# A hybrid attention and convolution layer on one core: the depthwise convolution in three half-length parts, and the work around it moved

## The chip, the cores and the metric

The kernel runs on one core of one Trainium2 chip, as one program. The metric is the device time of one execution in microseconds (us); a kernel's time is the median of several runs. TensorE (PE) does the matrix products, VectorE (DVE) and ScalarE (ACT) the elementwise work, GpSimd (POOL) small scalars, and SyncE (SP) issues most of the DMAs.

## The reference

One encoder layer is applied to two sequences that share weights: the prompt with 512 tokens and the sample with 256, both of width 1024. Half of the mixer is an attention with low-rank query and key/value projections (8 heads, 64 plain and 32 rotated dimensions), the other half a convolution over 512 channels:

```python
u = conv_a * jax.nn.sigmoid(conv_g)
u = lax.conv_general_dilated(u, dw_w[:, None, :], window_strides=(1,),
                             padding=[(CONV_PAD, CONV_PAD)],      # 15 on both sides
                             dimension_numbers=("NWC", "WIO", "NWC"),
                             feature_group_count=CONV_CH) + dw_b  # 31 taps, one filter per channel
u = jax.nn.silu(layer_norm(u, conv_ln_g, conv_ln_b))
merged = jnp.concatenate([rms_norm(attn, attn_out_g), rms_norm(u, conv_out_g)], axis=-1)
...
x = x + merged @ w_out
x = x + swiglu(rms_norm(x, norm2_g), w_gate, w_up, w_down)        # 2816 wide
return rms_norm(x, final_g)
```

## The kernel before

The 768 tokens are six blocks of 128: 0 to 3 the prompt's, 4 and 5 the sample's. Every value that enters a matrix product is split into a rounded high part, cast by ACT, and a low remainder, subtracted by DVE (`split`); three products of halves make one, all issued through the helper `mm`.

The order of work. The kernel is written for a scheduler that places each instruction on its engine by program order as priority, as soon as its inputs and buffers allow by its own estimate; an instruction in `tc.keep_in_program_order` (`pinned` while `pin[0]` is set) is not moved past others of its kind. Each engine then runs its list strictly in order. Buffers come from pools; a pool with `reuse="tile"` lets a new tile wait only for the old tiles that lie in the same memory, one without it for the whole old pool.

The stages, with their time in the profiled execution:

- 0 to 116 us, projection for the convolution: TensorE makes `pc`, in four channel groups of 128; `glu` turns a group into `u`, with padding of zeros at both ends, for each sequence.
- 116 to 161 us, the other projections: queries, keys, values. A query block's rotated dimensions are turned by `rope` on DVE (four instructions a block, into scratch tiles `rc` and `rs` and back to the query tile `sa`).
- 161 to 268 us, attention in 12 units, four pairs of heads for the sample and eight heads for the prompt; `unit_step(i)` overlaps the steps of neighbouring units. The steps are: transposed and split queries (`ptq`, then `qh` by ACT and `ql` by DVE), scores `pss`, row maxima `ngmx` by DVE, the exponential by ACT, transposed probabilities `ptp`, output `po`, `attnT`.
- In between the convolution's taps run on DVE, a multiply-add per tap on a whole row of tokens (`acc<-u,c,acc`). They are not written where they run: `mm` hands some out for every product that it issues, at a rate for each stage (`RATE`).
- After unit `LN0` = 4 come the prompt's convolution norms: `conv_ln` (transposes `pcl`, statistics on DVE, result `z` by ACT), `conv_act1` and `conv_act2` (transposes `pca`, tanh, row sums `prc`), `conv_split`. The attention's own norm is `attn_norm` (transposes `pan` and `pcb`).
- 268 to 303 us, the convolution half of the output projection, `oc(b, o)` for prompt block b and half o (`pe`). The sample's taps, norms and activation stand between these products.
- 303 to 361 us, the attention half, block by block (`both`, `out_attn`), and each block's norm (`x1_norm`) and transposes (`x1_turn`).
- 361 to 812 us, the feed-forward network; the last of its down products that shares a pattern is `p4`. To 843.5 us, a last product (`hd`) and the final norm. The last product's weights `w` arrive in `sr` tiles; ACT casts them to `ra` and `sa` regions, in the same list as `p4`'s casts `wr<-sr`.

Of the kernel before, what the change touches and what calls it, by code (L numbers as in the profile page):

```python
# [27 lines left out]
KW = 31  # L28
# [21 lines left out]
def tile_hybrid_layer(  # L50
# [53 lines left out]

    def split(dst_hi, dst_lo, src, scale=None):
        if scale is None:
            ACT.copy(dst_hi, src)  # L107
            DVE.tensor_sub(dst_lo, src, dst_hi.bitcast(F32))  # L108
# [67 lines left out]
    def wab(cols=1024):  # L176
# [10 lines left out]
    acc = [[accp.tile([128, n], F32, tag=f"acc{s}{i}", name=f"acc{s}{i}") for i in range(4)] for s, (_, n) in enumerate(SEQ)]  # L187
    u = [
        [up.tile([128, n + 2 * PAD], F32, tag=f"u{s}", name=f"u{s}{i}", bufs=4) for i in range(4)]
        for s, (_, n) in enumerate(SEQ)  # L190
    ]
    for s, (_, n) in enumerate(SEQ):
        for t in u[s]:
            POOL.memset(t[:, :PAD], 0.0)
            POOL.memset(t[:, PAD + n :], 0.0)
# [3 lines left out]
    def conv_chunk(i, j):  # L199
# [8 lines left out]
    slab = [  # L208
        [acc[s][k // 2] if k % 2 else u[s][k // 2][:, PAD : PAD + n] for s, (_, n) in enumerate(SEQ)]
        for k in range(8)  # L210
    ]
# [36 lines left out]

    def conv_taps(i, s):

        w = lambda j: c[:, C_DW + i * KW + j : C_DW + i * KW + j + 1]
        n = SEQ[s][1]
        a, us = acc[s][i], u[s][i]
        ACT.activation(a, us[:, :n], AF.Identity, bias=c[:, C_DB + i : C_DB + i + 1], scale=w(0))
        for j in range(1, KW):
            yield n / 512, lambda j=j: DVE.scalar_tensor_tensor(a, us[:, j : j + n], w(j), a, ALU.mult, ALU.add)  # L256
# [49 lines left out]
    def glu(i):  # L306
        for s, (o, n) in enumerate(SEQ):
            t1 = ta.tile([128, 512], F32, tag="t1", name=nm("t1"), bufs=2)
            t2 = ta.tile([128, 512], F32, tag="t2", name=nm("t2"), bufs=2)
            DVE.tensor_mul(t1[:, :n], pcs[i][1][s], rb[:, o : o + n])  # L310
            ACT.activation(t1[:, :n], t1[:, :n], AF.Tanh)
            DVE.tensor_mul(t2[:, :n], pcs[i][0][s], rb[:, o : o + n])
            DVE.scalar_tensor_tensor(
                u[s][i][:, PAD : PAD + n], t1[:, :n], 1.0, t2[:, :n], ALU.add, ALU.mult
            )
            taps[s].append(conv_taps(i, s))
# [54 lines left out]
    def rope(dst, src, b, n, tp):  # L371
# [3 lines left out]
        tcs = tp.tile([128, n, 2, 16], F32, tag=f"rc{n}", name=nm("rc"), bufs=2)  # L375
        tsn = tp.tile([128, n, 2, 16], F32, tag=f"rs{n}", name=nm("rs"), bufs=2)
# [88 lines left out]
    def q_up(b):  # L465
# [9 lines left out]
        for n in range(2):  # L475
            ACT.activation(qt[b][:, n * 384 : (n + 1) * 384], pp[n][:, :384], AF.Copy, scale=fq[:, b : b + 1])
        qr = qt[b].rearrange("p (h d) -> p h d", h=H)[:, :, DN:]
        rope(qr, qr, b, H, cTp)
# [90 lines left out]
    cz = {}  # L569

    def conv_ln(b):
# [12 lines left out]
        z = up.tile([128, CC], F32, tag="u0", name=nm("z"), bufs=4)  # L584
# [558 lines left out]
    gw[0] = wx, wpair(gs[0][:, KB])
    x1_turn(5)
    x1_turn(2)
    out_attn(3, 1, wa[1])
    prep(1)
    x1_norm(3)
    behind = {0: lambda: t_sums(2), 1: lambda: t_sums(0), 2: lambda: t_split2(1), 3: lambda: t_split2(2), 4: lambda: t_split2(0)}
    for f in range(NFILL):  # L1150
# [6 lines left out]
        if f == 0:  # L1157
            x1_turn(3)
# [181 lines left out]
    al, wl = [], []  # L1340
    ra_ = region("ra", 12288, F32R)
    sas = [region(f"sa{i}", NSA, F32R) for i in range(2)]
    wat = [ra_[:, NP * 768 + i * 512 : NP * 768 + (i + 1) * 512] for i in range(7)] + [sa(i * 512, 512) for i in range(15)]
    for q in range(NQ):
        w = w_load(1, 0, q)
        for f, i in pairs(q):
# [4 lines left out]
            tc.keep_in_program_order(ACT.copy(wl[f][0], w[:, i, :]))  # L1351
            DVE.tensor_sub(wl[f][1], w[:, i, :], wl[f][0].bitcast(F32))
# [114 lines left out]
```

## Time and profile before

| | us |
|---|---|
| median of 3 runs (lowest to highest) | 846.23 (844.44 to 848.56) |
| profiled execution | 845.27 |
| its span, first to last instruction | 843.5 |
| mean granted clock of TensorE | 0.986 |
| busy: PE / DVE / ACT / POOL | 813.0 / 716.3 / 435.2 / 74.0 |

Busy time is the time in which an engine has an instruction under way. The granted clock is the share of TensorE's full clock that it was given. What an engine waited for is inferred from the events that released it. TensorE's share of 96% is an average over stages of different kinds; what matters for a change in one stage is what the engines do there.

### The profile page before, as it was taken

The numbers are of one execution on the slowest core, as the hardware profiler recorded it, in microseconds if no ns is written. First come the engines' busy times: TensorE is split into PE (matmuls) and PEld (weight loads), VectorE is DVE, ScalarE is ACT, GpSimd is POOL, SyncE is SP. The second block draws the span as 40 slices with busy tenths as digits, with TensorE's granted clock in tenths as the row PEclk, the third lists the DMA queues.
The fourth block names the chain that finished last, engine by engine and source line by source line (L and its number), as shares of the span: only waits on it lengthen the run. The fifth ranks groups of instructions, "written<-read, shape, count | busy, mean of one in ns | idle before, by whom it ended". The sixth has DMA issues, their size and how long they took to land.

```text
span 843.5 us, 12569 instructions
## 1 busy us (share of the span) xinstructions
PE 813.0 (96%) x4414; PEld 727.1 (86%) x4414; DVE 716.3 (85%) x1314; ACT 435.2 (52%) x888; POOL 74.0 (9%) x111
## 2 busy tenths in 40 slices
PE   7999999799999899999999999999999999999996
PEld 6889998676766678799999999999999988888876
DVE  6499999988689965898999888898988669989985
ACT  7633347678686254784333343433434346456734
POOL 0000430002010201100000000000000000004602
PEclk9999999989799999999999999999999999999999
DMA  8822102300001231368554333444344699963334
GB/s 307 295 62 63 45 20 80 128 1 1 1 1 51 75 101 75 114 204 287 193 193 151 117 127 135 147 143 148 126 150 142 207 328 313 315 199 117 133 113 150
DMA packets 50928, 117.20 MB, mean 139 GB/s; under 512 B 5297, under 2 KB 19761, under 8 KB 50865
## 3 DMA queue, kind: packets, MB, share of 16 engines
q1 hardware_dynamic: 50288, 115.80, 40.7%
q8 instruction: 35, 0.57, 0.3%
q10 hardware_dynamic: 576, 0.59, 0.2%
q14 instruction: 29, 0.23, 0.1%
HBM read 93.96 MB, written 22.41 MB: 138 GB/s over the span
## 4 chain that ended last, share of the span: by engine, by line
PE 78%; DVE 9%; ACT 6%; issue 4%; DMA 2%; POOL 1%; ACTq 0%; POOLq 0%; DVEq 0%
PE bank L299 55%; PE pc L299 8%; PE pss L299 3%; DVE acc L256 3%; PE po L299 3%; PE pq L299 2%; PE pt L299 2%; PE ptp L737 2%; DVE wr L108 1%; ACT ra L463 1%; DMA sr<-wdn 1%; ACT ra L107 1%; ACT sa L720 1%; DVE sa L111 1%; PE ptq L692 1%
## 5 line engine op out<-in xcount | busy, mean ns | idle before, releaser
L299 PE MATMUL bank<-ra,wr 128*128 128x384 f32 x1056 | 186.6, 336 | 0.0
L299 PEld LDWEIGHTS bank<-ra,wr 128*128 128x128 f32 x1056 | 183.4, 188 | 0.0
L299 PE MATMUL bank<-sa,wr 128*128 128x384 f32 x780 | 139.2, 336 | 0.0
L299 PE MATMUL bank<-wr,wr 128*128 128x512 f32 x594 | 135.4, 389 | 1.7 <-ACT wr L107 1.5
L299 PEld LDWEIGHTS bank<-sa,wr 128*128 128x128 f32 x780 | 135.5, 188 | 0.0
L299 PEld LDWEIGHTS bank<-wr,wr 128*128 128x128 f32 x594 | 111.4, 188 | 25.4 <-ACT wr L107 1.9
L256 DVE SCALAR_TENSOR_TENSOR acc<-u,c,acc 128x512 f32<-128x512 f32 (+1 forms) x240 | 132.8, 609 | 0.1
L107 ACT CAST wr<-vt 128x512 fp32r<-128x512 f32 x88 | 54.6, 621 | 101.1 <-PE bank L299 98.5
L107 ACT CAST wr<-sr 128x512 fp32r<-128x512 f32 x106 | 64.8, 617 | 63.5 <-PE bank L299 60.4
L108 DVE TENSOR_TENSOR wr<-sr,wr 128x512 fp32r<-128x512 f32 x106 | 71.7, 680 | 16.5 <-ACT wr L107 16.5
L1246 POOL TENSOR_SCALAR fme<-fms 128x1 f32<-128x1 f32 x6 | 24.6, 4107 | 418.7 <-ACT vt L1236 418.5
L108 DVE TENSOR_TENSOR wr<-vt,wr 128x512 fp32r<-128x512 f32 x88 | 59.9, 682 | 0.0
L299 PE MATMUL pc<-ra,sa 128*128 128x512 f32 (+1 forms) x288 | 53.6, 347 | 5.9 <-ACT ra L110 5.9
L299 PEld LDWEIGHTS pc<-ra,sa 128*128 128x128 f32 x288 | 45.5, 194 | 13.0 <-ACT ra L110 6.4
L107 ACT CAST wr<-ra 128x384 fp32r<-128x384 f32 x51 | 26.1, 512 | 34.9 <-PE bank L299 19.9
L299 PE MATMUL pss<-ra,qh 96*128 96x512 f32 (+1 forms) x96 | 31.3, 413 | 7.3 <-ACT qh L107 6.0
L108 DVE TENSOR_TENSOR wr<-ra,wr 128x384 fp32r<-128x384 f32 x51 | 28.2, 553 | 9.1 <-ACT wr L107 8.0
L299 PE MATMUL bank<-wr,ra 128*128 128x512 f32 x144 | 34.8, 396 | 0.0
L299 PE MATMUL pq<-sa,ra 128*128 128x384 f32 x108 | 33.9, 341 | 0.0
L717 DVE TENSOR_REDUCE ngmx<-pss 128x1 f32<-128x512 f32 (+1 forms) x40 | 27.0, 685 | 6.4 <-PE pss L299 6.2
L299 PEld LDWEIGHTS bank<-wr,ra 128*128 128x128 f32 x144 | 26.6, 187 | 6.3
L720 ACT ACTIVATE sa<-pss,ngmx 128x512 f32<-128x512 f32 (+1 forms) x48 | 29.3, 620 | 2.2 <-PE ptp L737 1.9
(234 smaller groups left out, 1343.9 us busy)
## 6 DMA issues: line engine op xcount, KB each, us to landing
sr<-wgu SPq DMA_DIRECT2D x52, 512.0 KB, 4.0
sr<-wdn SPq DMA_DIRECT2D x34, 512.0 KB, 4.6
sumd<-xall SPq DMA_DIRECT2D x44, 192.0 KB, 1.9
ra<-sumd SPq DMA_DIRECT2D x44, 192.0 KB, 5.0
actd<-xall SPq DMA_DIRECT2D x11, 384.0 KB, 2.3
xall<-actd SPq DMA_DIRECT2D x11, 384.0 KB, 2.9
st<-wconv SPq DMA_DIRECT2D x7, 512.0 KB, 5.5
xr<-xtok SPq DMA_DIRECT2D x6, 512.0 KB, 4.4
```

Of the source, the lines that this page charges most:

```text
L107: ACT.copy(dst_hi, src)
L108: DVE.tensor_sub(dst_lo, src, dst_hi.bitcast(F32))
L111: DVE.scalar_tensor_tensor(dst_lo, src, scale, dst_hi.bitcast(F32), ALU.mult, ALU.subtract)
L256: yield n / 512, lambda j=j: DVE.scalar_tensor_tensor(a, us[:, j : j + n], w(j), a, ALU.mult, ALU.add)
L299: pinned(PE.matmul(out, lhsT, rhs, start=start, stop=stop))
L463: ACT.copy(t[DN:DQ, h, :], t[DN:DQ, 0, :].bitcast(F32))
L692: PE.transpose(pt[:DQ, o : o + 128], qt[b0 + b][:, h * DQ : (h + 1) * DQ], ident)
L717: DVE.tensor_reduce(mx, ps.rearrange("p (j n) -> p j n", j=m), AX.X, ALU.max, negate=True)
L720: ACT.activation(P[:, js], ps[:, js], AF.Exp, bias=ngmx[:, b0 + b, h : h + 1], accum_out=asum[:, b0 + b, h : h + 1],)
L737: PE.transpose(pt[:, o : o + 128], P[b][:, j * n + kt * 128 : j * n + (kt + 1) * 128], ident)
L1246: POOL.tensor_scalar(fme[b], fms[:, 2 * b + 1 : 2 * b + 2], 1.0, EPS, ALU.mult, ALU.add)
```

## The change

It has six parts.

1. The convolution. A group's row `u` is now stored as two half-length rows, the even and the odd tokens (`u0` and `v1`), both sequences side by side in one tile `uv`. With even taps, odd taps and their sums `cab`, three half-length filters give P (16 taps on `u0`), Q (15 on `v1`) and S (15 on `u0+v1`); even outputs are P + Q, odd ones S - P - Q shifted. The first tap of each is ACT's. The rates are changed with it, and at most 2 instead of 4 taps' worth are handed out at once (`TAPW`).
2. The norms start after unit 7 instead of 4 and follow in consecutive units, the sample's included, which was between the output projections.
3. `q_rope` of the prompt's blocks is written after units 0 and 1 instead of before the first.
4. Five pools of the attention stage get `reuse="tile"`.
5. The blocks after the mixer run 4 0 1 2 5 3 instead of 4 0 1 5 2 3.
6. The splits of the last product's weights are issued after the last cast of `p4`.

```diff
-RATE = {"A": 0.6, "B": 1.4, "C": 0.6, "D": 1.0, "S": 1.0, "F": 1.2}
+RATE = {"A": 0.6, "B": 1.25, "C": 0.3, "D": 1.1, "S": 1.0, "F": 1.2}
-TAPW = 4
-LN0 = 4
+TAPW = 2
+TAPC = 0.81
+LN0 = 7
...
-    def conv_taps(i, s):
-        a, us = acc[s][i], u[s][i]
-        ACT.activation(a, us[:, :n], AF.Identity, bias=..., scale=w(0))
-        for j in range(1, KW):
-            yield n / 512, lambda j=j: DVE.scalar_tensor_tensor(a, us[:, j : j + n], w(j), a, ALU.mult, ALU.add)
+    def conv_taps(i):
+        u0, v1 = half_rows(i, 0), half_rows(i, 1)
+        P, Q, S = pqs[:, :NP_], pqs[:, HP : HP + NP_ - 1], pqs[:, 2 * HP : 2 * HP + NP_ - 1]
+        yield TAPC, lambda: DVE.tensor_add(xs, u0, v1)
+        ACT.activation(P, u0[:, :NP_], AF.Copy, scale=w(0))
+        ACT.activation(Q, v1[:, 1:NP_], AF.Copy, scale=w(1))
+        ACT.activation(S, xs[:, 1:NP_], AF.Copy, scale=ab(0))
...
+        for j in range(1, 16):
+            yield TAPC, lambda j=j: tap(P, u0, j, w(2 * j))
+            if j < 15:
+                yield TAPC, lambda j=j: tap(Q, v1, 1 + j, w(2 * j + 1))
+            yield TAPC, lambda j=j: tap(S, xs, 1 + j, ab(j))
+        yield TAPC, lambda: DVE.tensor_sub(S, S, P[:, 1:])
+        for s, (o, n) in enumerate(SEQ):
+            r = acc[s][i].rearrange("p (n two) -> p n two", two=2)
+            def even():
+                DVE.scalar_tensor_tensor(r[:, :, 0], Q[:, m : m + h], db, P[:, m : m + h], ALU.add, ALU.add)
+            def odd():
+                DVE.scalar_tensor_tensor(r[:, :, 1], S[:, m : m + h], db, Q[:, m : m + h], ALU.add, ALU.subtract)
...
+        if b >= 4:
+            q_rope(b)
...
-    atp, at_close = pool("atp")
+    atp, at_close = pool("atp", reuse="tile")          # tmp, dp, psD, psX as well
...
         unit_step(i)
+        if i < 3:
+            for b in (2 * i, 2 * i + 1) if i < 2 else ():
+                q_rope(b)
...
         elif i == LN0 + 2:
             for k in range(4):
                 conv_act1(0, k)
                 conv_act2(0, k)
-            for b in range(NB):
-                load_x(b)
-        elif i == LN0 + 4:
+            pin[0] = True
+            conv_ln(4)
+            conv_ln(5)
+            pin[0] = False
+        elif i == LN0 + 3:
+            conv_split(0)
+            for k in range(4):
+                conv_act1(1, k)
+                conv_act2(1, k)
             attn_norm(4)
             attn_norm(5)
-            conv_split(0)
-        elif i == LN0 + 7:
+        elif i == LN0 + 4:
             wc0 = conv_w(0)
...
-    oc(0, 1)
-    tap_all(1)
-    oc(1, 1)
-    conv_ln(4)
-    conv_ln(5)
-    oc(2, 1)
-    for k in range(4):
-        conv_act1(1, k)
-    oc(3, 1)
-    for k in range(4):
-        conv_act2(1, k)
-    conv_split(1)
+    for b in range(4):
+        oc(b, 1)
...
+    behind_p4 = last_act[0].ins
...
-            tc.keep_in_program_order(ACT.copy(wl[f][0], w[:, i, :]))
-            DVE.tensor_sub(wl[f][1], w[:, i, :], wl[f][0].bitcast(F32))
+            with tc.issue_after(behind_p4):
+                split(wl[f][0], wl[f][1], w[:, i, :])
```

What this does to the engines' lists is seen at three places. The first is DVE's list just ahead of the first `ql`, the low half of the first transposed queries. `acc<-u` are taps of whole rows, `pqs<-` half-length taps; `rc`, `rs` and, in the new kernel, `st` are the scratch of a rotation, and `sa` the query tile that it turns. Before:

```order
L256 SCALAR_TENSOR_TENSOR acc_114<-u_122,c,acc_114 128x512
L381 TENSOR_TENSOR rc_1738<-sa_160_1418,c 128x256
L382 TENSOR_TENSOR rs_1739<-sa_160_1418,c 128x256
L256 SCALAR_TENSOR_TENSOR acc_115<-u_123,c,acc_115 128x512
L383 TENSOR_TENSOR sa_160_1418<-rc_1738,rs_1739 128x8x16
L384 TENSOR_TENSOR sa_160_1418<-rc_1738,rs_1739 128x8x16
L256 SCALAR_TENSOR_TENSOR acc_115<-u_123,c,acc_115 128x512
L256 SCALAR_TENSOR_TENSOR acc_116<-u_124,c,acc_116 128x256
L108 TENSOR_TENSOR ql_1785<-ptq_1779,qh_1784 96x512
L108 TENSOR_TENSOR ql_1798<-ptq_1792,qh_1797 96x512
```

The same place now, with the sixth rotation still around the first two `ql`:

```order
L446 TENSOR_TENSOR sa_168_1433<-st_1884 128x8x16
L447 TENSOR_TENSOR sa_168_1433<-st_1884 128x8x16
L290 SCALAR_TENSOR_TENSOR pqs_1578<-uv_114,c,pqs_1578 128x400
L290 SCALAR_TENSOR_TENSOR pqs_1841<-xs_1840,cab,pqs_1841 128x400
L290 SCALAR_TENSOR_TENSOR pqs_1578<-xs_1577,cab,pqs_1578 128x400
L444 TENSOR_TENSOR st_1889<-sa_168_1433,c 128x256
L445 TENSOR_TENSOR st_1889<-sa_168_1433,c 128x256
L290 SCALAR_TENSOR_TENSOR pqs_1841<-uv_115,c,pqs_1841 128x401
L111 TENSOR_TENSOR ql_1777<-ptq_1771,qh_1776 96x512
L111 TENSOR_TENSOR ql_1790<-ptq_1784,qh_1789 96x512
L446 TENSOR_TENSOR sa_168_1433<-st_1889 128x8x16
```

The rotations keep their place, though they are written later; the taps between them are shorter.

The second place is TensorE's list at the end of the convolution half of the output projection, `pe`, up to the first `bank` products. Before, the sample's activation and row sums stand in it:

```order
L299 MATMUL pe_3037<-sa_386_2834,ra_69 128x512 x12
L596 MATMUL pca_3051<-ident,z_3018 128x128
L596 MATMUL pca_3051<-ident,z_3035 128x128
...
L596 MATMUL pca_3075<-ident,z_3035 128x128
L299 MATMUL pe_3082<-sa_386_2834,ra_69 128x512 x12
L299 MATMUL prc_3096<-ones,th_3055 128x2 x4
L299 MATMUL prc_3096<-ones,th_3070 128x2 x4
L299 MATMUL bank_3122<-sa_376_2734,ra_69 128x512 x12
```

Now, with `pcb` the last transposes of an attention norm:

```order
L737 MATMUL pcb_2994<-ident,z_2972 128x128 x4
L737 MATMUL pcb_3007<-ident,z_2972 128x128 x4
L353 MATMUL pe_3020<-sa_411_2893,ra_69 128x512 x12
L353 MATMUL pe_3034<-sa_411_2893,ra_69 128x512 x12
L353 MATMUL pe_3048<-sa_411_2893,ra_69 128x512 x12
L353 MATMUL pe_3062<-sa_411_2893,ra_69 128x512 x12
L353 MATMUL bank_3081<-sa_401_2817,ra_69 128x512 x12
```

The sample's norm and activation have moved into attention, and the projections follow each other.

The third place is ACT's list near the end of `p4`; `wr<-sr` and `wr<-act` are casts for `p4`, `ra<-sr` for the last product. Before:

```order
L107 CAST wr_3211<-act_3940 128x384
L1351 CAST ra_7426<-sr_3217 128x512 x2
L107 CAST wr_3213<-sr_3218 128x512
L107 CAST wr_3215<-act_3940 128x384
L107 CAST wr_3203<-act_3940 128x384
L107 CAST wr_3201<-sr_3219 128x512
L107 CAST wr_3207<-act_3940 128x384
L1351 CAST ra_7426<-sr_3218 128x512 x2
L107 CAST wr_3205<-sr_3219 128x512
L107 CAST wr_3209<-sr_3220 128x512
```

Now:

```order
L110 CAST wr_3160<-sr_3178 128x512
L110 CAST wr_3166<-act_3899 128x384
L110 CAST wr_3164<-sr_3178 128x512
L110 CAST wr_3168<-sr_3179 128x512
L110 CAST ra_7385<-sr_3176 128x512 x2
L110 CAST ra_7385<-sr_3177 128x512 x2
L110 CAST sa_482_7386<-sr_3178 128x512 x2
```

Both pairs of `ra<-sr` casts have moved behind `p4`'s last cast.

More of the change, by code (lines that the diff above doesn't have):

```diff
@@ L185, in tile_hybrid_layer, with half_rows @@
     psA, psA_close = pool("psA", bufs=8, space=PSUM)
[L187 to L195, printed above, removed]
+    HL = [n // 2 + 16 for _, n in SEQ]
+    HO = [0, HL[0]]
+    HW = sum(HL)
+    uv = [accp.tile([128, 2 * HW], F32, tag=f"uv{i}", name=f"uv{i}") for i in range(4)]
+    acc = [[t[:, o : o + n] for t in uv] for o, n in SEQ]
+    HP = 401
+    def half_rows(i, w):
+        return uv[i][:, w * HW : (w + 1) * HW]
     hT = rtiles()
@@ L206, in tile_hybrid_layer @@
     wc[0, 0] = w0
[L208 to L211, printed above, removed]
+    place = [stg.tile([128, 1024], F32, tag="st", name=nm("st"))]
+    place += list(uv)
+    place += [up.tile([128, 3 * HP], F32, tag="pqs", name=nm("xs"), bufs=2) for _ in range(2)]
+    slab = [[p[:, o : o + n] for o, n in SEQ] for p in place]
     t0 = stg.tile([128, 1024], F32, tag="st", name=nm("st"))
@@ L218, in tile_hybrid_layer @@
             nc.sync.dma_start(t0[:, ks], wconv[0, 0][:, ks])
+        if k == 7:
+            p = stg.tile([128, 1024], F32, tag="st", name=nm("st"))
+            slab.append([p[:, o : o + n] for o, n in SEQ])
         for s, (o, n) in enumerate(SEQ):
@@ L226, in tile_hybrid_layer @@
             split(hT[s][0][:, k, :], hT[s][1][:, k, :], slab[k][s], g1[:, k : k + 1])
+    for t in uv:
+        t2_ = t.rearrange("p (w n) -> p w n", w=2)
+        for lo_, hi_ in ((0, 8), (HL[0] - 8, HL[0] + 8), (HW - 8, HW)):
+            POOL.memset(t2_[:, :, lo_:hi_], 0.0)
     wc[1, 0] = conv_chunk(1, 0)
@@ L247, in build_rb @@
             ACT.activation(rb[:, o : o + n], pr[s][:, :n], AF.Copy, scale=0.5)
[L249 to L256 removed]
+    cab = cpool.tile([128, 4, 16], F32, name="cab")
@@ L312, in glu @@
             DVE.tensor_mul(t2[:, :n], pcs[i][0][s], rb[:, o : o + n])
[L313 to L316, printed above, removed]
+            pair = lambda t, w: t[:, :n].rearrange("p (n two) -> p n two", two=2)[:, :, 1 - w]
+            for w in range(2):
+                DVE.scalar_tensor_tensor(
+                    half_rows(i, w)[:, HO[s] + 8 : HO[s] + 8 + n // 2], pair(t1, w), 1.0, pair(t2, w), ALU.add, ALU.mult
+                )
+        taps[0].append(conv_taps(i))
     WTN = [960] * 4 + [768] * 2
@@ L374, in rope @@
         sn = c[:, None, C_SIN + b * 16 : C_SIN + (b + 1) * 16].to_broadcast([128, 2 * n, 16])
-        tcs = tp.tile([128, n, 2, 16], F32, tag=f"rc{n}", name=nm("rc"), bufs=2)
-        tsn = tp.tile([128, n, 2, 16], F32, tag=f"rs{n}", name=nm("rs"), bufs=2)
+        if tp is None:
+            t_ = stg.tile([128, 1024], F32, tag="st", name=nm("st"))
+            tcs, tsn = [
+                t_[:, i * n * 32 : (i + 1) * n * 32].rearrange("p (n two f) -> p n two f", two=2, f=16)
+                for i in range(2)
+            ]
+        else:
+            tcs = tp.tile([128, n, 2, 16], F32, tag=f"rc{n}", name=nm("rc"), bufs=2)
+            tsn = tp.tile([128, n, 2, 16], F32, tag=f"rs{n}", name=nm("rs"), bufs=2)
         s4 = src.rearrange("p n (two f) -> p n two f", two=2)
@@ L569, in tile_hybrid_layer, with z_tile @@
     cz = {}
+    zt = []
+    def z_tile():
+        if not zt:
+            t = up.tile([128, 3 * HP], F32, tag="pqs", name=nm("z"), bufs=2)
+            zt.extend([t[:, : CC], t[:, CC : 2 * CC]])
+        return zt.pop(0)
     def conv_ln(b):
@@ L843, in tile_hybrid_layer @@
         elif i == LN0 + 1:
+            pin[0] = True
             conv_ln(2)
             conv_ln(3)
+            pin[0] = False
+            for b in range(NB):
+                load_x(b)
         elif i == LN0 + 2:
```

52 lines of the change are left out of this document (36 added, 16 removed).

## Prediction

> **What bounds the kernel now.** First the busy line of the page, then the busy time of each engine in stretches cut where the work changes (columns: time, length, then busy microseconds of PE, PEld, DVE, ACT and POOL with their instructions, granted clock, DMA share, GB/s).
>
> ```profile
> PE 813.0 (96%) x4414; PEld 727.1 (86%) x4414; DVE 716.3 (85%) x1314; ACT 435.2 (52%) x888; POOL 74.0 (9%) x111
> 116.00:161.00 45.00, 44.50 (x258) 41.66 (x257) 43.19 (x84) 36.67 (x85) 6.69 (x8) 1.00 0.30 106
> 161.00:176.00 15.00, 7.93 (x42) 6.85 (x41) 13.15 (x27) 4.99 (x15) 0.00 (x0) 0.77 0.00 1
> 176.00:194.70 18.70, 18.29 (x122) 12.18 (x119) 17.50 (x36) 15.62 (x47) 0.00 (x0) 1.00 0.00 1
> 194.70:220.00 25.30, 24.16 (x149) 17.56 (x147) 21.68 (x46) 20.41 (x44) 4.60 (x12) 1.00 0.00 1
> 220.00:232.40 12.40, 11.81 (x44) 9.03 (x45) 7.30 (x16) 8.15 (x19) 1.30 (x2) 0.59 0.01 1
> 232.40:267.70 35.30, 35.22 (x187) 21.12 (x185) 31.89 (x66) 30.25 (x69) 2.60 (x4) 1.00 0.09 31
> 267.70:303.00 35.30, 30.72 (x159) 24.23 (x159) 29.48 (x66) 13.76 (x34) 5.79 (x14) 1.00 0.14 45
> 303.00:308.00 5.00, 5.00 (x16) 3.94 (x15) 3.89 (x8) 4.36 (x8) 1.59 (x2) 0.66 0.42 120
> 308.00:361.00 53.00, 50.94 (x250) 42.09 (x249) 36.94 (x59) 27.79 (x61) 6.71 (x12) 1.00 0.30 109
> 361.00:769.00 408.00, 408.00 (x2231) 392.23 (x2230) 354.98 (x637) 178.63 (x324) 0.00 (x0) 1.00 0.57 191
> 769.00:812.00 43.00, 41.30 (x182) 33.62 (x181) 41.14 (x73) 28.66 (x63) 24.64 (x6) 1.00 0.32 104
> ```
>
> TensorE bounds it: 96% busy overall, without a gap in the 408 us of FFN that the change doesn't touch. Its matmuls are the same after the change, so what can be won is time in which PE is idle or at half clock, and that lies in 161 to 361: idle 7.07 at 161-176 (15.00 - 7.93), 0.41, 1.14, 0.59, 0.08, 4.58 in the output projection's conv half (267.7-303), 0, then 2.06. The clock takes, as busy time times one less the granted clock, 11.81 x 0.41 = 4.8 at 220-232, 5.00 x 0.34 = 1.7 at 303-308, and about 2.4 near 170 (some 5 us of work at half speed). All of it is 25 us, with 1.7 more at 769-812: the ceiling of the gain is 27 us, or 819.
>
> What PE waited for, from the waits (total, times, longest) and the order in time:
>
> ```profile
> ACT qh L107 <- DVE sa L384: 6.2, 1, 6.2
> PE pss L299 <- ACT qh L107: 6.0, 2, 5.7
> 162.45 1.08 PE L692 MATMUL ptq<-ident,sa 128*96 128x128 f32 x8 [0.96 <-ACT sa L476]
> 169.23 1.65 PE L299 MATMUL pss<-ra,qh 96*128 96x256 f32 x6 [5.70 <-ACT qh L107]
> 289.92 1.86 PE L576 MATMUL pcl<-ident,acc 128*128 128x128 f32 x8 [1.22 <-DVE acc L256]
> 295.32 0.33 PE L596 MATMUL pca<-ident,z 128*128 128x128 f32 x1 [0.80 <-ACT z L585]
> 296.19 0.98 PE L596 MATMUL pca<-ident,z 128*128 128x128 f32 x7 [0.55 <-ACT z L585]
> 299.79 0.95 PE L299 MATMUL prc<-ones,th 128*128 128x2 f32 x8
> 300.98 0.61 PE L299 MATMUL prc<-ones,th 128*128 128x2 f32 x4 [0.24 <-ACT th L612]
> 302.20 0.61 PE L299 MATMUL prc<-ones,th 128*128 128x2 f32 x4 [0.62 <-ACT th L612]
> ```
>
> So DVE is late twice: at the first scores (pss) of attention, behind rotations and taps in its queue, and in the output projection, where the sample's taps, LN and activation stand between projections.
>
> **Part 1, the half-length convolution.** Tap prices, by form and, back to back, from the chain:
>
> ```profile
> L256 DVE SCALAR_TENSOR_TENSOR acc<-u,c,acc 128x512 f32<-128x512 f32 x120 | 83.1, 743 | 0.1
> L256 DVE SCALAR_TENSOR_TENSOR acc<-u,c,acc 128x256 f32<-128x256 f32 x120 | 49.9, 475 | 0.0
> 137.56 2.65 DVE acc L256 x4
> 203.28 2.38 DVE acc L256 x6
> L313 DVE SCALAR_TENSOR_TENSOR u<-t,t 128x512 f32<-128x512 f32 x4 | 2.7, 686 | 0.2
> L313 DVE SCALAR_TENSOR_TENSOR u<-t,t 128x256 f32<-128x256 f32 x4 | 1.7, 416 | 0.0
> ```
>
> Back to back a 512-column tap costs 2.65/4 = 0.663 us and a 256-column one 2.38/6 = 0.397, so 1.04 ns a column, and a 401-column tap 0.397 + 145 x 0.00104 = 0.548. Before: 120 x 0.663 + 120 x 0.397 = 127.2 us. After: 4 x 44 = 176 half-length taps = 96.4; 4 sums u0+v1 and 4 subtractions at about 0.5 = 4.0; per group four combinations, 2 of 256 and 2 of 128 columns (0.397 and 0.26) = 1.3, together 5.3; the GLU's second store per tile adds a fixed part, 8 x about 0.1 = 0.8 (its two rows above: 270 ns for 256 columns, so some 146 ns fixed busy, less when queued); tap sums 0.2. Together 106.7, so DVE has 20.5 us less to do. The strided writes of GLU and combinations are in no row; between 0 and double price that is 0 to +8 us of DVE; I take no extra, since the strided rotation writes and reads run beside plain ones at the usual slope. The three ACT starts of 401 columns per group instead of two, and the pad fills on POOL, lie on engines at 52% and 9%.
>
> This is off the path wherever PE doesn't wait. By the order of DVE's instructions, ahead of the first `ql` stand before 118 taps of 512 columns and 1 of 256 (78.6 us), after 131 half taps (71.8), but also 4 sums, 2 subtractions, half the combinations, the GLU's 0.8 and 0.2 (together 6.7), and 5 1/2 rotation pairs instead of 6 (0.4 less). The net is only 0.5 less: the lowered rates of the earlier stages eat the saving by taking fewer taps there, none is left over at the first scores. In the middle of the stage the balance is up to 1.0 against, where PE has 0.5 us of idle in 45. Gain at the first scores: 0.5, between -1.0 and 6 (all the stall).
>
> **Part 2, norms one unit later, and the sample's conv work moved into attention.** DVE needs from the first `ql` to the last combination 10 `ql` and 24 score maxima, 45 half taps (24.7), 2 subtractions (1.0) and 8 combinations (2.6).
>
> ```profile
> L717 DVE TENSOR_REDUCE ngmx<-pss 128x1 f32<-128x512 f32 x32 | 21.7, 685 | 5.3 <-PE pss L299 5.1
> L108 DVE TENSOR_TENSOR ql<-ptq,qh 96x512 fp32r<-96x512 f32 x12 | 8.1, 682 | 3.2 <-ACT qh L107 3.2
> ```
>
> The 34 others at 0.685 x 0.663/0.743 = 0.61 make 20.8, the sum 49.1. From about 169 this is 218, at the earliest, for the LN transposes `pcl(0)` to have their last channel group; before they ran at 194.7. PE has, up to that place in its new order, two units' more work, and the LN transposes and activations that stood there have moved behind; before, PE was busy from 169.2 to 220 for about 5.9 + 18.29 + 24.16 = 48.4, which is 46 at full clock; less some 4 for the transposes that moved behind (32 at 0.13) and some 4 more, since the new place lies a few score groups past 220, it is 46 again, with 2.4 of half clock after the stall: it arrives at about 217. `pcl` is pinned, and behind it in PE's queue stand the next scores, so what DVE is late PE stands still: DVE was 94% busy at 176-194.7, and 49.1/0.94 = 52 gives 221. So a new wait of 1 to 5 us; I take 3.
>
> From there to the first output-projection matmul little DVE work is left. After that matmul PE has the projection, and between its tiles no LN, activation or row sums (the rows at 289.9 to 302.2 above, 5.3 us of matmuls, move ahead into attention). Idle there was 4.58; the waits for LN, activation and row sums go, part of the `pan`/`pcb` waits (about 1) stays: gain 3.6, between 2 and 4.6.
>
> ACT gets denser instead: between `pcl(0)` and the last attention tile it has all LN outputs, activations and softmaxes, where DVE's lag no longer spreads them. At 194.7-267.7 it was busy 20.41 + 8.15 + 30.25 = 58.8 us of 73; less the 20.4 that now lies ahead and with about half of the 13.76 of 267.7-303 added, 45 us of ACT work have some 47 us of PE time. I charge 1 us, between 0 and 6.
>
> The half clock of 220-232 (4.8) comes without an idle stretch, where row sums of two columns, transposes and half-waiting `po` follow each other. These now come later and closer. Nothing says that they disappear: I keep 4.8, between 0 and 9.6.
>
> [...]
>
> First scores to bank stage then: -0.5 (stall) + 3 (new wait) - 3.6 (projection) + 1 (ACT) = -0.1; against it the idle and queueing of 176-220 (0.41 + 1.14) and of DVE-late scores, gone once taps are through, at most 1.5 + 0.6. I take -2.0. And since PE now comes to the bank stage out of uninterrupted projections, not out of idle bits and row sums, the half clock at 303-308 goes: -1.7, between -1.7 and 0. Together -3.8.
>
> **Part 3, deferred rotations.** In program order four blocks' rotations now stand behind the first units, but the order on DVE keeps all but the second half of one ahead of the first `ql`, as before: they are needed by the first units, and DVE had room earlier. They use staging tiles; a weight load that waits for one costs nothing seen at a DMA share of 0.00 to 0.01 up to 232. Zero; the stall of 5.70 stays.
>
> **Part 4, pools that wait by tile.** No row separates a wait for a pool's release. Attention tiles could begin before the last C tile is freed, at most the 0.96 before `ptq`: 0, between 0 and 1.
>
> **Part 5, blocks 4 0 1 2 5 3.**
>
> ```profile
> 351.31 1.09 PE L988 MATMUL bank<-ident,vt 128*128 128x128 f32 x8 [1.56 <-ACT vt L979]
> 359.97 1.09 PE L988 MATMUL bank<-ident,vt 128*128 128x128 f32 x8 [0.51 <-ACT vt L979]
> ```
>
> The transposes of a normed block waited 1.56 and 0.51 for ACT's norm. Each now stands a product later: -1.0, between -2.06 (all idle of 308-361) and +1.
>
> **Part 6, early casts at the end.**
>
> ```profile
> 807.56 1.14 ACT L1351 CAST ra<-sr 128x512 fp32r<-128x512 f32 x2 [2.81 <-DMA sr<-wdn]
> 808.60 1.13 ACT L107 CAST wr<-sr 128x512 fp32r<-128x512 f32 x2
> 809.25 0.69 DVE L108 TENSOR_TENSOR wr<-sr,wr 128x512 fp32r<-128x512 f32 x1 [1.62 <-ACT wr L107]
> 809.27 0.50 PE L299 MATMUL bank<-wr,wr 128*128 128x512 f32 x1 [1.47 <-ACT wr L107]
> 809.99 4.19 PE L299 MATMUL bank<-wr,wr 128*128 128x512 f32 x17 [0.22 <-DVE wr L108]
> ```
>
> PE waits 1.47 + 0.22 for a cast of p4's weights that stands behind two `ra<-sr` casts of the last product, and these wait for a load. With the two (1.14 us) and their wait moved behind, PE can win 1.69 at most; p4's own cast also needs its load, so -1.0, between -1.7 and +0.5 (if the moved casts then hold up the last product, which begins 4 us later).
>
> **The sum.** -3.8 (parts 1 and 2) + 0 + 0 - 1.0 - 1.0 = -5.8. On the profiled execution's 845.27 this is 839.5; that execution lies 0.96 under the median of 846.23, so the median would be 840.4. I take 840.
>
> **The rivals.**
> 1. Large gain: the first scores no longer wait (5.7 and 2.4 of half clock), and the spell of 220-232 goes (4.8). For it: 20.5 us less of DVE work before 218. Against: the order has DVE only 0.5 us lighter at the first `ql`. Then 5.8 + 12.9 = 18.7 less: 827.
> 2. No change: the projection's 3.6 is won, and lost again at the pinned `pcl` (5) and to ACT (2): 844 to 846. For it: 49.1 us of DVE work against 46 of PE.
> 3. Slower: ACT becomes the bound of the last five units. From `pcl(0)` at 221 its 45 us at the 86% at which it ran in 232.4-267.7 are 52.5, PE is done 5.5 later than its own 47, and the spell of half clock that such waits feed doubles (4.8). 840.4 + 5.5 + 4.8 = 850.7. It decides from ACT over 90% busy in the 50 us behind `pcl(0)`, with PE's idle released by ACT.
> [...]
>
> **How the numbers follow.** The forecast (835 to 842) has a chance of 0.45, the large gain (822 to 835) 0.22, no change 0.20 and slower 0.13. The range leaves out a part of the large gain and of the slowest: 824 to 850. About 0.5%, 4.2 us, is what a measurement of this kernel can tell from no change: faster means under 842.0, which is 0.64; slower over 850.5, 0.11; the rest 0.25.
>
> **What would show it.** DVE's busy time falls by about 20 us and PE's stays near 805 to 813. First scores still wait near 169. `pcl` waits for DVE near 218 to 221. From the first projection matmul to the bank stage PE runs with under 1.5 us idle, and the bank stage begins at 299 to 301 instead of 302.7. The clock is 1.00 at the bank's start. No `ra<-sr` cast stands before p4's weights. I am wrong if the first scores come before 166, if PE idles on ACT after `pcl`, or if the clock's cost differs from the 8.9 us of before by over 4.

## The result: slower, and where the time went

The changed kernel takes 853.95 us (median of five executions) against 846.23, a ratio of 1.0073 with a 95% interval of 1.005 to 1.0095. One of the five ran in a slow state, at 1156.24 us and a granted clock of 0.652; the ratio leaves it out, and the median of the other four is 853.25. The forecast was 840. Its profiled span is 852.2 us, 8.7 more than before's 843.5.

The page of the changed kernel, its busy lines; VectorE has 20.3 us less to do than before, and TensorE is busy for 7 us longer with the same 4414 matmuls:

```profile
PE 820.0 (96%) x4414; PEld 732.5 (86%) x4414; DVE 696.0 (82%) x1284; ACT 435.5 (51%) x892; POOL 83.7 (10%) x107
```

The same stretches as in the prediction, of the changed kernel:

```profile
161.00:176.00 15.00, 9.57 (x52) 8.77 (x52) 13.28 (x34) 7.82 (x21) 0.00 (x0) 0.84 0.33 105
176.00:194.70 18.70, 18.22 (x114) 12.94 (x113) 16.73 (x30) 14.12 (x43) 0.00 (x0) 0.95 0.09 29
194.70:220.00 25.30, 25.30 (x140) 16.88 (x136) 22.91 (x41) 19.61 (x48) 0.00 (x0) 1.00 0.00 1
220.00:232.40 12.40, 7.35 (x32) 4.16 (x32) 11.33 (x26) 2.47 (x5) 2.03 (x6) 0.73 0.01 1
232.40:267.70 35.30, 31.20 (x144) 23.64 (x142) 15.65 (x29) 23.92 (x52) 3.82 (x10) 0.74 0.00 0
267.70:303.00 35.30, 32.88 (x169) 22.01 (x169) 18.13 (x32) 26.18 (x59) 6.12 (x15) 0.87 0.19 60
303.00:308.00 5.00, 5.00 (x28) 4.21 (x27) 4.05 (x8) 3.60 (x9) 1.48 (x4) 1.00 0.31 105
308.00:361.00 53.00, 53.00 (x249) 43.54 (x248) 32.12 (x50) 20.95 (x44) 4.05 (x8) 1.00 0.22 80
769.00:812.00 43.00, 43.00 (x191) 35.63 (x190) 41.70 (x74) 28.88 (x64) 24.81 (x4) 1.00 0.38 123
```

In 220 to 232.4 TensorE now idles for 5 us with VectorE busy nearly throughout, and to 303 the clock is far below full. From 303 on there is neither idle nor half clock.

Cut by landmarks of the work, one stretch runs from the first transposed queries (`ptq`) to the first `bank` product, the next from there to the feed-forward network. First the two of before, then the two of the changed kernel:

```profile
162.50:302.70 140.20, 127.30 (x689) 90.50 (x689) 119.35 (x247) 91.48 (x221) 14.29 (x32) 0.94 0.06 19
302.70:390.00 87.30, 85.24 (x433) 75.28 (x434) 68.68 (x113) 53.41 (x109) 8.29 (x14) 0.98 0.45 157
```

```profile
164.30:317.40 153.10, 135.62 (x689) 97.16 (x688) 106.45 (x195) 98.72 (x233) 13.45 (x34) 0.87 0.14 45
317.40:400.80 83.40, 83.33 (x434) 74.21 (x433) 61.59 (x100) 46.60 (x97) 6.91 (x12) 1.00 0.38 134
```

Attention with the projection's conv half is 12.9 us longer, although VectorE does 12.9 us less in it; the stage behind is 3.9 shorter. Up to `ptq` the changed kernel is 1.8 later, which lies within what the first stages differ between profiles of one code (162.5 to 165.8 for before's). The feed-forward network to the first matmul of the last product takes 421.9 (400.8 to 822.7) instead of 424.0 (390.0 to 814.0), and the end is the same 29.5. So 1.8 + 12.9 - 3.9 - 2.1 = 8.7.

Inside the long stretch, the waits of TensorE (total, times, longest), its list at the transposes `pcl`, and the end of VectorE's taps:

```profile
PE pcl L651 <- DVE uv L307: 4.4, 2, 3.4
PE pss L353 <- DVE ql L111: 4.3, 1, 4.3
PE pss L353 <- ACT sa L795: 2.7, 2, 1.6
```

```profile
222.08 0.64 PE L767 MATMUL ptq<-ident,sa 128*96 128x128 f32 x4
223.69 0.30 PE L651 MATMUL pcl<-ident,uv 128*128 128x128 f32 x1 [0.97 <-DVE uv L307]
227.40 1.30 PE L651 MATMUL pcl<-ident,uv 128*128 128x128 f32 x5 [3.40 <-DVE uv L307]
...
226.76 0.75 DVE L307 SCALAR_TENSOR_TENSOR uv<-pqs,c 128x256 f32<-128x256 f32 x2
```

TensorE comes to the transposes of the third group at 222.7 and of the fourth at 224.0; VectorE writes the last of the convolution just before 227.4. The clock in three stretches after that:

```profile
226.00:238.00 12.00, 9.93 (x30) 5.04 (x30) 6.99 (x16) 5.98 (x13) 2.03 (x6) 0.59 0.01 1
250.00:271.00 21.00, 18.30 (x74) 14.39 (x76) 7.57 (x15) 11.90 (x24) 4.04 (x8) 0.59 0.00 1
280.00:288.00 8.00, 7.06 (x28) 4.83 (x28) 3.21 (x7) 5.88 (x13) 1.69 (x4) 0.57 0.00 0
```

As busy time times one less the clock, these cost 4.1, 7.5 and 3.0 us. Such a stretch at half clock is called a spell below.

### The profile page after: what moved, and what is told of

The parts are those of the page before. It is cut to its first block, busy times and chain, and to the rows that moved or that the text cites. A ratio compares the mean times of both kernels' runs of the same rounds, so it can differ in the third digit from the quotient of the medians.

```text
span 852.2 us, 12548 instructions
## 1 busy us (share of the span) xinstructions
PE 820.0 (96%) x4414; PEld 732.5 (86%) x4414; DVE 696.0 (82%) x1284; ACT 435.5 (51%) x892; POOL 83.7 (10%) x107
## 4 chain that ended last, share of the span: by engine, by line
PE 84%; ACT 6%; DVE 4%; issue 3%; POOL 2%; DMA 1%; ACTq 0%; POOLq 0%; DVEq 0%
PE bank L353 58%; PE pc L353 8%; PE pss L353 3%; PE pe L353 3%; PE po L353 2%; PE pq L353 2%; DVE pqs L290 2%; PE ptp L812 2%; PE pt L353 1%; PE prc L353 1%; ACT ra L526 1%; ACT ra L569 1%; POOL r L151 1%; ACT sa L795 1%; PE ptq L767 1%
## 5 line engine op out<-in xcount | busy, mean ns | idle before, releaser
L110 ACT CAST wr<-vt 128x512 fp32r<-128x512 f32 x88 | 54.5, 621 | 89.4 <-PE bank L353 83.4
L1324 POOL TENSOR_SCALAR fme<-fms 128x1 f32<-128x1 f32 x6 | 38.9, 6481 | 415.4 <-ACT vt L1314 415.1
L290 DVE SCALAR_TENSOR_TENSOR pqs<-uv,c,pqs 128x401 f32<-128x401 f32 (+1 forms) x116 | 68.3, 629 | 0.1
L290 DVE SCALAR_TENSOR_TENSOR pqs<-xs,cab,pqs 128x400 f32<-128x400 f32 x60 | 36.4, 629 | 0.2 <-ACT pqs L286 0.2
L353 PE MATMUL pss<-ra,qh 96*128 96x512 f32 (+1 forms) x96 | 33.1, 423 | 3.0 <-ACT sa L795 2.7
```

Source lines behind the costliest of these rows:

```text
L110: last_act[0] = ACT.copy(dst_hi, src)
L290: DVE.scalar_tensor_tensor(d, x[:, o : o + n], sc, d, ALU.mult, ALU.add)
L353: pinned(PE.matmul(out, lhsT, rhs, start=start, stop=stop))
L1324: POOL.tensor_scalar(fme[b], fms[:, 2 * b + 1 : 2 * b + 2], 1.0, EPS, ALU.mult, ALU.add)
```

## The experiments

Theory A: the pinned transposes `pcl` stand too early in TensorE's list for the taps, which end near 227 us; TensorE runs out of other work there, and what follows (half clock, a chain of norm and activation that starts late) comes from that. Theory B: the norm and activation work packed into the last units is dear by itself, for ScalarE and the clock. Runs were timed beside the kernel before on the same chip; its medians there were 847.55, 847.44, 847.39 and 846.39.

### The parts that won (e1)

```diff
 # on the kernel before: both(2) and both(5) exchanged with their x1_turn and x1_norm,
+            with tc.issue_after(behind_p4):
+                split(wl[f][0], wl[f][1], w[:, i, :])
```

> The kernel before with parts 5 and 6 alone (block order 4 0 1 2 5 3, casts of the last product behind p4). By the two traces the changed kernel lost 12.9 us between the first transposed queries and the bank products, and won 3.9 us in the bank stage and 2.1 us at the end of p4. If the two wins come from parts 5 and 6, this kernel wins 1.7 at the end and about 2 in the bank stage (the 1.7 of half clock there belongs to the projection ahead of it and stays): 842 to 843. If the wins only come from another arrival time, nothing: 846.

Measured: 843.84, ratio 0.994 (0.9913 to 0.9968).

```profile
165.80:306.10 140.30, 127.24 (x688) 90.51 (x688) 119.37 (x247) 91.28 (x221) 14.34 (x32) 0.94 0.06 20
306.10:391.30 85.20, 85.12 (x435) 75.48 (x435) 66.55 (x109) 51.97 (x106) 8.54 (x14) 0.98 0.46 153
```

The second stretch is 85.2 instead of 87.3, with no idle, and its half clock (0.98) stays; the first is unchanged. The network takes 422.1 (391.3 to 813.4) instead of 424.0. So in this profile the block order gives 2.1 and the moved casts 1.9; the two were not run one by one. The price of the casts isn't the same in every execution: e8 below has the old ones, and its network takes 422.2 as well (390.1 to 812.3), with no wait for `p4`'s cast.

### One unit later (e2), one more (e6)

```diff
-LN0 = 7
+LN0 = 8      # e6: LN0 = 9, with wc0 = conv_w(0) at the last step
```

> The changed kernel with the norms one unit later still (LN0 = 8). Theory A (the pinned transposes pcl stand too early in TensorE's list, TensorE waits 5.3 us for the last taps, and the half clock that follows the wait costs more): the taps end near 227 and TensorE reaches pcl later by a unit, some 9 us, so the wait goes, with 4 us of half clock: 844 to 848. Theory B (the last units are too full of norm and activation work for ScalarE and for TensorE's clock, whatever the taps do): one unit less to spread it over, the same or worse: 853 to 858.

Measured: 843.25, ratio 0.9929 (0.9901 to 0.9957), 10.7 us under the changed kernel's median.

```profile
165.80:306.40 140.60, 127.67 (x691) 91.62 (x689) 106.05 (x195) 98.63 (x233) 13.49 (x34) 0.94 0.15 49
306.40:389.70 83.30, 83.21 (x433) 74.14 (x432) 62.05 (x101) 47.01 (x98) 6.94 (x12) 1.00 0.38 133
```

No wait for the taps is left at `pcl`; the stretch falls from 153.1 to 140.6, with the same work in the same few units. That is theory A, with a time a little under its range.

> The changed kernel with the norms after unit 9 (LN0 = 9, the output weights' split moved ahead to the last unit). At LN0 = 8 no wait for taps was left, so Theory A sees nothing more to win: 843 to 847, as at LN0 = 8 or a little over. Theory B: each unit later packs the chain tighter, and the last units have no scores to fill it: 848 to 854.

Measured: 847.55, 0.9985 (0.996 to 1.001); the stretch takes 146.3. The time lies between the two ranges. Here B has its share: packed once more, the end of attention costs 5.7 us.

### Fewer taps at the old place (e3)

```diff
-            yield TAPC, lambda j=j: tap(S, xs, 1 + j, ab(j))
+            if i < 2:
+                yield TAPC, lambda j=j: tap(S, xs, 1 + j, ab(j))
```

> The changed kernel without the 28 taps of S in the last two channel groups (that part of the convolution is left out): 15 us less on VectorE, ahead of the transposes pcl, which stay after unit 7. Theory A: the taps end near 212, no wait at pcl, the half clock there goes as well: 843 to 847. Theory B: the stalls behind the transposes stay, only the 5 us wait becomes idle elsewhere: 850 to 854.

Measured: 844.48, 0.997 (0.9935 to 1.0005). The condition takes out 15 taps of VectorE in each of two groups, 30 in all and not 28, which is 16.4 us: S has 16 taps, not 15, and ScalarE does the first. The convolution is written by 210, and `pcl` runs at 221.4 without a wait:

```profile
221.43 1.04 PE L652 MATMUL pcl<-ident,uv 128*128 128x128 f32 x8
...
168.00:310.00 142.00, 128.65 (x689) 93.71 (x688) 89.97 (x165) 98.07 (x233) 13.52 (x34) 0.90 0.15 48
```

142.0 instead of 153.1: with LN0 = 7 kept, 11 of the 12.9 us go when the taps end early.

### The sample's norms put back (e4, e7)

```diff
-            conv_ln(4)
-            conv_ln(5)
...
+    oc(1, 1)
+    conv_ln(4)
+    conv_ln(5)
+    oc(2, 1)      # activation and row sums of the sample follow as before; e7: LN0 = 8 as well
```

> The changed kernel with the sample's norms and activation back between the output projections, where they stood before; the prompt's norms stay after units 7 to 9. Theory A: the wait for the taps at pcl stays with its half clock: 851 to 854. Theory B: ScalarE and the clock have less to carry in the last units, the half clock of 251 to 270 us shortens, and with VectorE free of taps the projection carries the sample's norms without the waits of before: 844 to 848.

Measured: 855.1, 1.0078 (1.005 to 1.0106); the stretch takes 151.6 and the bank stage 85.1. That is the changed kernel's own time: B, with 844 to 848, is out, and A's 851 to 854 is missed by 1.1.

> The changed kernel with LN0 = 8 and the sample's norms and activation between the output projections, where they stood before. Theory A: the sample's place is worth only the small waits on either side: 842 to 846. Theory B: attention's end gets lighter by 5.3 us of matmuls and as much of ScalarE's time, the half clock of 260 to 271 us goes: 838 to 841.

Measured: 846.67, 0.9992 (0.9968 to 1.0015), the stretch 142.9 and the bank stage 85.1 instead of 83.3. Over both expectations: the sample's place among the projections is worse than in attention by 3.4 us (medians) to 4.1 us (the two stretches), 1.7 of it the half clock at the bank stage's start (0.66 in its first 5 us).

### Later norms without the new convolution (e5)

```diff
 # on the kernel before
-LN0 = 4
+LN0 = 7      # attn_norm, conv_split and conv_w moved along
```

> The kernel before with the prompt's norms after units 7, 8 and 9 instead of 4, 5 and 6, and the rest of that chain moved with them; convolution, pools, block order and end as before. Theory A (only the late taps at the pinned transposes made the later norms dear): here the prompt's taps are done by 170 us, so no wait arises at the transposes, and the later norms cost nothing or a little: 844 to 848. Theory B (norm and activation work packed into the last units is dear by itself): 850 to 855.

Measured: 846.92, 0.9996 (0.9967 to 1.0024). The prompt's norms at the changed kernel's place cost nothing where the taps are early. TensorE does wait 3.6 us for taps in this kernel, but for the sample's, among the output projections. And the spell of the kernel before at 220 to 232 is not there: with all of the prompt's transposes and row sums between 200 and 285 the clock stays full.

```profile
200.00:285.00 85.00, 81.25 (x450) 55.72 (x449) 75.16 (x155) 62.85 (x137) 12.39 (x26) 1.00 0.11 32
```

### The convolution without parts 5 and 6 (e9)

```diff
 # on the changed kernel with LN0 = 8: both(5) ahead of both(2) again, and
-            with tc.issue_after(behind_p4):
-                split(wl[f][0], wl[f][1], w[:, i, :])
+            tc.keep_in_program_order(ACT.copy(wl[f][0], w[:, i, :]))
+            DVE.tensor_sub(wl[f][1], w[:, i, :], wl[f][0].bitcast(F32))
```

> The changed kernel with LN0 = 8 and with the old block order and the old end, so that parts 1 to 4 are left with their norms one unit later. If parts 5 and 6 carried the gain of LN0 = 8 (4 us in the kernel before), the convolution's 20 us less of VectorE work is worth nothing in time: 846 to 848, as the kernel before. If the convolution is worth something once it doesn't hold up the transposes: 843 to 845.

Measured: 847.71, 1.0001 (0.9977 to 1.0026). Parts 1 to 4 together, with their norms one unit later, are worth nothing that can be told within a quarter of a per cent. That the twenty microseconds less of VectorE work are worth nothing by themselves is likely but not shown, since parts 2 to 4 are in the same kernel. The bank stage has the old order's idle but full clock:

```profile
305.70:391.40 85.70, 83.64 (x434) 74.16 (x434) 64.24 (x105) 48.97 (x101) 6.72 (x12) 1.00 0.40 137
```

### The first wait moved (e10, e11)

```diff
-RATE = {"A": 0.6, "B": 1.25, "C": 0.3, "D": 1.1, "S": 1.0, "F": 1.2}
+RATE = {"A": 0.6, "B": 1.25, "C": 1.0, "D": 1.1, "S": 1.0, "F": 1.2}
...
+            if len(qsub) > 1:
+                with tc.issue_after(qsub[1].ins):      # the second ql
+                    issue()
...
+                with tc.issue_after(qsub[1].ins):
+                    q_rope(b)
```

> The changed kernel with LN0 = 8, in which the rotations of the prompt's blocks and the taps that are handed out in attention are kept behind the second ql on VectorE (12 taps and 3 rotations fewer ahead of it, about 10 us), rate C 1.0. If the wait of 4.3 us for ql at the first scores is worth its length and the half clock after it (1.9 us): 837 to 840. If VectorE's work up to the last tap bounds the stretch, the wait only moves to the transposes pcl, some 5 us: 843 to 847.

Measured: 846.64, 0.9986 (0.9964 to 1.0008). The wait at the first scores is gone, and the clock with it is full; the first row is LN0 = 8 as it was, the second this kernel:

```profile
161.00:176.00 15.00, 9.54 (x54) 8.76 (x54) 13.96 (x35) 7.77 (x17) 0.00 (x0) 0.86 0.34 106
```

```profile
161.00:176.00 15.00, 12.64 (x86) 11.10 (x84) 9.22 (x22) 10.75 (x26) 0.00 (x0) 1.00 0.11 35
...
PE pcl L656 <- DVE uv L307: 1.6, 1, 1.6
165.80:310.90 145.10, 130.65 (x690) 92.30 (x688) 108.06 (x203) 99.15 (x233) 14.33 (x34) 0.94 0.15 48
```

VectorE was idle for 5.8 of the 15 us, the taps end that much later, `pcl` waits again, and the stretch is 4.5 us longer. The order overshot what it was to test, but the wait did move to the place expected.

> The same with LN0 = 9, so that the transposes stand another unit later. If the first wait moved to the transposes at LN0 = 8, it should have no place here, and the kernel wins 4 to 6 us on LN0 = 9 alone (847.5): 841 to 844. If the packed end of attention is what bounds it then, no gain: 846 to 849.

Measured: 846.98, 0.9995 (0.9962 to 1.0028); the stretch takes 144.9 instead of e6's 146.3. No gain that can be told: the packed end bounds it.

### What brings the half clock (e8, e12)

```diff
 # e8, on the kernel before: row sums of the last channel group alone
+        if i < 3:
+            return
         for b in range(nb):
             mm(pr[:, 2 * b : 2 * b + 2], th[:, b * 128 : (b + 1) * 128], ones[:, :2], ...)
```

> The kernel before with the row sums (prc) of the last channel group alone, those of three of four groups are left out; on TensorE nothing else moves. It asks what sends the clock to half at 222 to 232 us, where TensorE has no idle of over 0.9 us. If the two-column row sums do it, the spell goes (4.8 us) with some 4 us of the matmuls: 836 to 839. If the transposes or nothing in particular does it, only the 4 us: 842 to 843.

Measured: 843.39, 0.9971 (0.9945 to 0.9997), 4.1 us under the kernel before. The spell is still there, 3 us later, and it begins ahead of any row sum:

```profile
220.00:225.00 5.00, 3.38 (x18) 2.25 (x16) 4.70 (x10) 5.00 (x13) 0.00 (x0) 0.98 0.00 0
225.00:230.00 5.00, 5.00 (x16) 2.98 (x15) 3.08 (x7) 2.46 (x5) 1.30 (x2) 0.50 0.01 3
```

```diff
 # e12, on the changed kernel, in conv_ln
+        if b == 0:
+            for _ in range(20):
+                pinned(PE.matmul(pt, kT[0][0][:, 0, :128], kT[0][0][:, 0, :], start=True, stop=True))
```

> The changed kernel with 20 more matmuls of 512 columns (about 4.5 us) ahead of the first transposes pcl, whose results are overwritten: TensorE works in the time in which it waited for the last taps, and nothing else is moved. If the wait itself brings the half clock that follows it (3.7 us at 225 to 240, and through it part of the later spell at 250 to 270), the clock stays at 1.00 there: 848 to 851. If the transposes and the row sums bring it whether TensorE waits or not, the time stays or grows a little: 854 to 857.

Measured: 853.43, 1.0073 (1.0046 to 1.01), the changed kernel's own time.

```profile
219.00:229.30 10.30, 10.24 (x55) 6.91 (x52) 10.30 (x24) 2.36 (x5) 0.00 (x0) 1.00 0.00 1
229.30:250.00 20.70, 17.84 (x96) 11.32 (x95) 11.76 (x22) 16.34 (x36) 4.03 (x12) 1.00 0.00 1
250.00:270.00 20.00, 17.30 (x78) 13.05 (x76) 8.65 (x16) 11.23 (x23) 4.12 (x7) 0.66 0.00 1
```

The extra matmuls fill the wait, and the clock stays at 1.00 until 250: with the wait of 4.4 us goes the half clock of 226 to 238. But the time doesn't fall. The stretch from `ptq` to `bank` takes 152.4 us (165.6 to 318.0) instead of 153.1, though the spell that is gone cost 4.1: TensorE idles for 2.9 us in 229.3 to 250 instead. Counted from `ptq`, the first row sums come only 1.3 us earlier (249.92 less 165.6, against 249.90 less 164.3). So TensorE's pace doesn't bound that part; the norm and activation do. In the changed kernel's chain of what ended last, in order of time:

```profile
238.85 1.29 DVE bst L654 x2
...
240.59 0.56 POOL r L151
...
248.18 0.67 ACT yt L683
...
249.90 1.07 PE prc L353 x8
```

It passes through VectorE's statistics, POOL's power and ScalarE's activations. So theory A stands as to the cause: where the taps end before TensorE comes to `pcl`, by a later place (e2) or by fewer taps (e3), 10.7 and 9.5 us of the median go. How a wait of 4.4 us comes to cost so much is not shown. It is not a late start of the chain alone: in e2 the last group's transposes come later after `ptq`, 68.4 us against 63.1, and what stands behind them takes 72.2 us against 90.0. First e2, then the changed kernel:

```profile
234.20:306.40 72.20, 66.18 (x353) 50.20 (x352) 45.08 (x80) 53.61 (x114) 13.49 (x34) 0.93 0.20 64
```

```profile
227.40:317.40 90.00, 82.81 (x394) 60.64 (x395) 49.43 (x87) 59.63 (x128) 13.45 (x34) 0.82 0.16 52
```

The changed kernel has 42 matmuls more left there, about as much idle (7.2 us against 6.0), and a clock of 0.82 instead of 0.93. My expectation of 848 to 851, which priced the first spell by itself, was wrong.

What sets off the later spell at 250 to 271 stays open. Its clock falls at 253, 0.5 us behind a wait of 1.10 us for ScalarE and ahead of one of 1.60. It comes with or without the first spell (0.59 in 250 to 271, and 0.66 in 250 to 270 of e12), and it is there in e3 at 246 to 263 (0.50 in 250 to 260) without any wait for taps.

## Why the prediction was wrong, step by step

**Part 1, right in VectorE's time.** DVE's busy time fell by 20.3 us (predicted 20.5), and a half tap costs 0.546 back to back (predicted 0.548):

```profile
215.72 5.46 DVE pqs L290 x10
```

The strided writes cost no more: a combination of 256 columns begins at 222.12 and the next tap at 222.51, 0.39 us later, where a plain tap of 256 columns took 0.397.

**The first scores, right.** `ql` still waits behind rotations and taps; TensorE has the high halves from 166.3 and then stands for 4.33 us until 172.0.

**Part 2, the step that failed: "a new wait of 1 to 5 us; I take 3", with the half clock kept at 4.8 and ScalarE charged 1.** The wait was named at the right place with the right cause. The taps ended at 227.4, not at 218 to 221: from the first `ql` (171.3, 2 us later than forecast) VectorE took 56 us against 49 to 52. Its work was counted rightly, 45 half taps and 50 us busy in all against 49.1; it was idle for 6 us, 4.7 of them in twelve waits for TensorE's scores, where the forecast allowed 3 (52 less 49.1):

```profile
171.30:227.40 56.10, 50.54 (x281) 34.97 (x281) 50.05 (x91) 36.56 (x99) 0.00 (x0) 0.93 0.04 12
DVE ngmx L792 <- PE pss L353: 4.7, 12, 1.0
```

TensorE came late too, to the fourth group at 224.0 (to the third at 222.7) and not at 217. The idle in 220 to 230, nearly all of it at `pcl`, was 4.8 (10.00 - 5.17):

```profile
220.00:230.00 10.00, 5.17 (x24) 2.92 (x22) 9.99 (x23) 1.23 (x3) 0.32 (x2) 0.78 0.00 0
```

That is within the bounds, with some luck: both ends of the difference had slipped by some 6 to 9 us. Mis-sized was what went with it. I priced the wait by its length, as if TensorE went on behind it at its old pace, and kept the half clock at 4.8, at most 9.6, twice that by my estimate. Behind the wait came three spells, which cost 14.6 us, and 7.2 us of idle (2.1, 2.7 and 2.4 to 250, 272 and 290):

```profile
228.50:250.00 21.50, 19.42 (x92) 12.18 (x91) 11.44 (x22) 15.70 (x34) 4.03 (x12) 0.83 0.00 1
250.00:272.00 22.00, 19.30 (x80) 14.67 (x80) 7.93 (x16) 12.90 (x26) 4.04 (x8) 0.61 0.00 1
272.00:290.00 18.00, 15.58 (x86) 11.54 (x83) 9.15 (x18) 15.85 (x40) 2.43 (x6) 0.81 0.04 14
290.00:317.40 27.40, 27.40 (x139) 21.15 (x138) 19.81 (x32) 15.17 (x31) 2.96 (x8) 1.00 0.50 160
```

The idle behind the wait is hardly new, e2 has 6.0 of it. Against e2 the stretch is 12.5 us longer: 4.6 more idle (17.5 against 12.9) and 8.0 more busy time for as many matmuls (135.62 against 127.67). So the runs put 9.5 to 12.5 us on the lateness (by medians 9.5 in e3 and 10.7 in e2, by stretches 11.1 and 12.5), against the 3 that I took. The clock is the term that was furthest off, though e12 shows that its first spell has no price by itself. Of the signs that I had named for being wrong, two came: TensorE idles on ScalarE after `pcl` (2.7 us at `pss`), and the clock costs over 4 more than the 8.9 of before. The projection's gain of 3.6 was real: 290 to 317.4 is busy throughout. It was won late and lost early.

The half clock of the kernel before didn't go with the number of transposes: there are 131 in the 44 us of 176 to 220, at a clock of 1.00, and 15 in 220 to 232.4, at 0.59.

**The slower rival had the wrong engine.** It asked for ScalarE over 90% busy behind `pcl(0)`; ScalarE was busy 15.70 of 21.50 and 12.90 of 22.00. VectorE's late taps decided, not the load of ScalarE.

**Parts 3 and 4** cannot be told from zero; e9 holds them with parts 1 and 2 and gives 1.0001.

**Parts 5 and 6 and the bank stage's clock, right in sign, too small.** Predicted -1.0 for the order, -1.0 for the casts and -1.7 for the clock; measured -3.9 in the bank stage for order and clock together, and -2.1 at the end. e9, with the old order and full clock, parts the 3.9: from 87.3 to its 85.7 is the clock, 1.6, and from there to 83.4 the order, 2.3. The clock's part goes with the sample's norms, since e7, which puts them back, has the half clock again. Against both stands the 12.9, predicted as -2.1.

**A version that beats both** is the changed kernel with LN0 = 8: 843.25, ratio 0.9929. By e1 and e9 its gain is that of parts 5 and 6; with them alone the kernel before takes 843.84.

## What to carry to other kernels

Work taken from VectorE, which isn't the bound here, bought 9.5 us where TensorE waited for its taps (30 taps, 16.4 us, in e3); 20 us less of it, with the parts that came with it and no wait for taps at `pcl`, gave a ratio of 1.0001 (e9). A pinned consumer that is moved must be placed by when the last producer really ends, its own waits included: one unit later made 10.7 us here. A wait of 4.4 us ahead of a chain through four engines went with a loss of 9.5 to 12.5 us, so its length was no measure of its price; how the rest comes about is not shown. The two small repairs gave 2.1 to 2.3 us (the block order) and 0 to 2 us (the casts, whose wait was missing in one profile of the old order).

## What the runs showed of the hardware

A wait of 4.4 us, 3.4 of it in one piece, was followed by half clock in the changed kernel (0.59 in 226 to 238), and with matmuls in its place the clock stayed at 1.00 in 219 to 250 (e12). The clock fell within the long piece, which ends at 227.4: it is 1.00 in 224 to 225, 0.84 in 225 to 226 and 0.50 in 226 to 227.4. The spell at 250 to 271 is not like it: the clock is 0.98 in 252.5 to 253 and 0.50 in 253 to 255, behind a wait of 1.10 us. The first scores show the like of the first spell: behind a wait of 4.3 us the clock in 161 to 176 is 0.86 (e2), and without that wait 1.00 (e10). For the spell of the kernel before, row sums of two columns are not the trigger: in e8 a score product already takes 0.63 us at 225.20, against 0.40 at 222.61, and the first row sums come at 225.63. Transposes stand more densely where its clock is full (131 in 44 us at 1.00, 15 in 12.4 us at 0.59). Nor does TensorE's list settle it: e2 and e9 run the same list at this place with nearly the same waits, 1.52 us at the longest in both, and only e9 falls to half clock (0.72 over the 12 us, against 1.00). First e2, then e9:

```profile
234.00:246.00 12.00, 8.72 (x53) 6.14 (x50) 9.90 (x19) 10.30 (x22) 4.04 (x12) 1.00 0.00 0
```

```profile
234.00:246.00 12.00, 9.61 (x42) 7.77 (x43) 8.61 (x18) 10.02 (x23) 4.04 (x12) 0.72 0.00 0
```

So a spell after short waits can come in one execution and not in another; what decides it stays open, and the price of a spell read from one profile is that of one execution.
